# Two more groups of a down projection by seven block products, and the up projection's products grouped by length

## The chip, the cores and the metric

One core of a Trainium2 chip. The metric is the device time in microseconds (us) of one execution of the whole two-layer trunk; the median of several runs counts.

## What is computed

Each of two layers projects the normalised input into three attention branches (stick-breaking, forgetting, and a sparse one over selected keys), gates and mixes them, and adds them to the residual stream. The change touches only what follows in each layer, the feed-forward part, and one load at the very end:

```
h2 = _rmsnorm(x, g_mlp)
x = x + jnp.square(jax.nn.relu(h2 @ w_up)) @ w_down
...
return _rmsnorm(x, g_final)
```

There are 256 tokens, 1024 model columns and 4096 hidden columns, all float32.

## The kernel before, in words

**Products.** A float32 operand is split into a rounded part (hi) and its rest (lo). ScalarE writes hi (L92) and VectorE subtracts it (L93); both results go into rings of four buffers each, `whi` and `wlo`, of 128 x 1024. A full product is `mm3` (L120 to L122): hi by hi, hi by lo and lo by hi, three matmuls. Weights arrive in a ring of four `raw` tiles of 1 MB, loaded by SyncE's queue.

**Up projection** (`up_mm`, L708 and L709). The 4096 hidden columns are taken in 16 groups c of 256, each of two blocks of 128. A block gets its own PSUM bank. For each of eight slices k of the contraction, the weight's hi multiplies the input's hi and lo at once (512 columns, L708), and the weight's lo multiplies the input's hi (256 columns, L709), added into the second half of the bank. Then `up_part` adds the two halves (ScalarE copies one, VectorE adds the other, L681) and applies relu and square; the bank is free when VectorE's L681 is done. `up_done` splits the result. Banks of the name `mm` are a ring of three; the first two groups take three `mm` and one `av`. Their order on TensorE is written out by hand (`manual_schedule`); everything else is put in order by a scheduler when the program is built, and each engine then runs its own queue strictly in that order.

**Down projection.** A group c < `NS` is done by `down_seven`: its 256 tokens x 256 hidden x 1024 columns are a product of 2 x 2 block matrices, done as seven block products (`ORDER`) in place of eight. For that, VectorE forms four sums of the activations in `up_done` (L694 to L697) and splits a 128 x 896 tile (L702), and in `down_seven` forms four combinations of the weights in a tile `T` (L754 to L756), of which there is one buffer, and then splits seven half-rows of 512 columns where an ordinary group has four. The seven sums are gathered in banks p1 to p7 by all groups. The other groups are done by `down_half`, four slices of 128 and 512 output columns at a time: column half 0 goes into banks p4 and p2, half 1 into p8 and p3. I call a `down_seven` call a **seven** (21 matmuls of 512 columns) and a `down_half` call a **half** (24 of them).

```
items = sorted([((c + 0.5) / NS, down_seven, (c,)) for c in range(NS)] +
               [((q + 1) / (8 - NS // 2), down_half, (q, 0)) for q in range(8 - NS // 2)], key=lambda t: t[0])
```

This list is the first pass: with `NS = 6`, six sevens and the five halves of column half 0, interleaved by their fractions. Then `down_sum` combines p1 to p7 on ScalarE and VectorE while TensorE runs the halves of column half 1, and the last lines add to the residual, square it for the final norm, scale and store. `gfb`, the final gain, is loaded in the last layer just before the first pass.

Of the kernel before, what the change touches and what calls it, by code (L numbers as in the profile page):

```python
# [9 lines left out]
F32 = mybir.dt.float32  # L10
# [5 lines left out]
T, D, DEPTH, COLS, DFF = 256, 1024, 2, 7244, 4096  # L16
# [5 lines left out]
EPS = 1e-6  # L22
NEG = -1.0e38
GONE = -3.0e38
NS = 6
TWO_PI = 6.283185307179586


def AP(src, off, dims):
    return bass.AP(tensor=src.tensor, offset=src.offset + off, ap=[list(d) for d in dims])  # L30
# [3 lines left out]
def trunk_kernel(ctx: ExitStack, tc: tile.TileContext, x, positions, g_mix, w_in, b_forget, w_branch,  # L34
                 w_out, g_mlp, w_up, w_down, g_final, out):
    nc = tc.nc
    act, dve, pool, pe, dma = nc.scalar, nc.vector, nc.gpsimd, nc.tensor, nc.sync
# [3 lines left out]
    tp2 = ctx.enter_context(tc.tile_pool(name="t2", bufs=1))  # L41
# [6 lines left out]
    def at_tile(name="at"):  # L48
        return ps.tile([128, 512], F32, name=name, tag="at", bufs=2)
# [35 lines left out]
    def split(raw, k, n, steps=1):  # L85
        hi = wp.tile([128, 1024], F32R, name="whi", tag="whi", bufs=4)
        lo = wp.tile([128, 1024], F32R, name="wlo", tag="wlo", bufs=4)
        h3 = hi[:, :k * n].rearrange("p (k n) -> p k n", k=k)
        l3 = lo[:, :k * n].rearrange("p (k n) -> p k n", k=k)
        m = k // steps  # L90
        for i in range(0, k, m):
            act.activation(h3[:, i:i + m], raw[:, i:i + m], AF.Copy)  # L92
            dve.tensor_sub(l3[:, i:i + m], raw[:, i:i + m], h3[:, i:i + m].bitcast(F32))  # L93
        return h3, l3

    def raw_tile(k, n):
        raw = wp.tile([128, 2048], F32, name="raw", tag="raw", bufs=4)
        return raw[:, :k * n].rearrange("p (k n) -> p k n", k=k)

    def w_rows(src, off, rs, k0, n, loads=1):  # L100

        raw = raw_tile(4, n)
        m = 4 // loads
        for i in range(0, 4, m):
            dma.dma_start(raw[:, i:i + m, :], AP(src, off + (k0 + i) * 128 * rs, [[rs, 128], [128 * rs, m], [1, n]]))
        r = []
        for q in range(2):
            h, l = split(raw[:, 2 * q:2 * q + 2, :], 2, n, 2 if loads == 4 and q == 0 else 1)
            r += [(h[:, i, :], l[:, i, :]) for i in range(2)]
        return r  # L110
# [7 lines left out]
    def mm3(o, a, b, start, stop):  # L118
        (ah, al), (bh, bl) = a, b
        pe.matmul(o, ah, bh, start=start, stop=False)  # L120
        pe.matmul(o, ah, bl, start=False, stop=False)  # L121
        pe.matmul(o, al, bh, start=False, stop=stop)  # L122
# [9 lines left out]
    def blk(tiles, k, c0=0, c1=256, p0=0, p1=128):  # L132
        h, l = tiles[k // 2][:2]
        return h[p0:p1, k % 2, c0:c1], l[p0:p1, k % 2, c0:c1]
# [50 lines left out]
    def rstd_of(ss):  # L185
        n = ss.shape[1]
        ms = small.tile([128, 2], F32, name="ms")[:, :n]
        pool.tensor_add(ms, ss[:, :, 0], ss[:, :, 1])  # L188
        pool.tensor_scalar(ms, ms, 1.0 / D, EPS, op0=OP.mult, op1=OP.add)
        r = small.tile([128, 2], F32, name="rstd")[:, :n]  # L190
        pool.tensor_tensor(r, ms, mhalf[:, :n], op=OP.pow)
        return r
# [25 lines left out]
    for layer in range(DEPTH):  # L218
# [8 lines left out]
        with tc.tile_pool(name=f"att{layer}", bufs=1, reuse_waits="tile") as att:  # L227
# [110 lines left out]
            for n, c in enumerate((KI, KC, KC + 64)):  # L338
# [3 lines left out]
                p = at_tile("kT")  # L342
                for j in range(2):
                    pe.transpose(p[:, j * 128:j * 128 + 128], kdup[:, j, n, :], ident)
                hi, lo = kh[:, n, :], kl[:, n, :]
# [12 lines left out]
            for j, c, n in SEG:  # L358
                for h in range(4):
                    z = at_tile("zi")  # L360
                    i = h % 2
# [56 lines left out]
            p = at_tile("cum")  # L418
# [10 lines left out]
            p = at_tile("cumt")  # L429
# [238 lines left out]
        with tc.tile_pool(name=f"mlp{layer}", bufs=1, reuse_waits="tile") as mlp:  # L668
            sq, uT = {}, {}
# [15 lines left out]
            def up_done(c):  # L685

                u = sq[c]
                if c >= NS:
                    hi, lo = [mlp.tile([128, 2, 256], F32R, name=f"u{t}{c}") for t in "hl"]
# [14 lines left out]
            def up_mm(o, wb, ks):  # L704

                h, l = wb
                for k in ks:
                    pe.matmul(o, h[:, k, :], xt[k // 2][2][:, :, k % 2, :], start=k == 0, stop=False)  # L708
                    pe.matmul(o[:, 256:512], l[:, k, :], blk(xt, k)[0], start=False, stop=k == 7)  # L709

            first = []
# [2 lines left out]
            for ks in (range(4), range(4, 8)):  # L714
                for n, (o, w) in enumerate(first):
                    up_mm(o, w, ks)
                    if n == 0 and not ks[0]:
                        part(1)
                    if ks[0]:
                        up_part(n // 2, n % 2, [o])  # L720
                        if n % 2:
                            up_done(n // 2)
# [19 lines left out]
            def add(p, a, b, stop):  # L742
                if p not in prod:
                    prod[p] = BANK[p](f"p{p}")
                mm3(prod[p], a, b, p not in opened, stop)
                opened.add(p)

            def down_seven(c):

                raw = raw_tile(2, 1024)  # L750
                dma.dma_start(raw, AP(w_down, (layer * DFF + c * 256) * D, [[D, 128], [128 * D, 2], [1, D]]))
                r4 = raw.rearrange("p k (h n) -> p k h n", h=2)
                t = mlp.tile([128, 4, 512], F32, name="T", tag="T", bufs=1)
                dve.tensor_sub(t[:, 0:2], r4[:, :, 1, :], r4[:, 0])  # L754
                dve.tensor_sub(t[:, 2], r4[:, 1, 1, :], t[:, 0])
                dve.tensor_sub(t[:, 3], r4[:, 1, 0, :], t[:, 2])  # L756
                right = []
                for v in (r4[:, 0, 0:1, :], r4[:, 1], t[:, 0:2], t[:, 2:4]):
                    k = v.shape[1]
                    h, l = split(v, k, 512)  # L760
                    right += [(h[:, i], l[:, i]) for i in range(k)]
                hi, lo = uT[c]
                for p, f, w in ORDER:
                    add(p, (hi[:, f], lo[:, f]), right[w], c == NS - 1 and p in (1, 5, 6, 7))

            def down_half(q, cg):

                c = NS + 2 * q
                ws = w_rows(w_down, layer * DFF * D + cg * 512, D, 2 * c, 512)
                end = c == 14  # L770
                order = [(i, j) for i in range(4) for j in range(2)]
                if end and cg and layer == DEPTH - 1:
                    order = [(i, j) for j in range(2) for i in range(4)]
                for i, j in order:
                    add(((4, 2), (8, 3))[cg][j], blk(uT, 2 * c + i, j * 128, j * 128 + 128), ws[i], end and i == 3)

            def down_sum():

# [12 lines left out]

            last = layer == DEPTH - 1
            if last:
                gfb = mlp.tile([128, D], F32, name="gfb")
                dma.dma_start(gfb, AP(g_final, 0, [[0, 128], [1, D]]))
                ss = small.tile([128, 2, 2], F32, name="ss")
            else:
                xt, ss, part = norm_in(layer * 8 + 8, (at_tile, pt_tile))
            items = sorted([((c + 0.5) / NS, down_seven, (c,)) for c in range(NS)] +
                           [((q + 1) / (8 - NS // 2), down_half, (q, 0)) for q in range(8 - NS // 2)], key=lambda t: t[0])  # L800
            for _, f, args in items:
                f(*args)
            for cg in range(2):
                if cg == 0:
                    down_sum()
                else:
                    for q in range(8 - NS // 2):
                        down_half(q, 1)
                    o = prod[8], prod[3]
                for j in range(2):  # L810
                    if cg:
                        dve.scalar_tensor_tensor(xs[j][cg], o[j], r2[:, j:j + 1], xs[j][cg], op0=OP.mult, op1=OP.add)
                    if last:
                        junk = small.tile([128, 512], mybir.dt.bfloat16, name="junk", tag="junk", bufs=1)
                        act.activation(junk, xs[j][cg], AF.Square, accum_out=ss[:, j, cg:cg + 1])
                        dve.tensor_mul(xs[j][cg], xs[j][cg], gfb[:, cg * 512:cg * 512 + 512])
                if not last:
                    part(cg)
                for j in range(2):
                    if last and cg == 1:  # L820
                        rl = rstd_of(ss[:, j:j + 1, :])
                        act.activation(xs[j][1], xs[j][1], AF.Copy, scale=rl)
                        dma.dma_start(AP(out, j * 128 * D + 512, [[D, 128], [1, 512]]), xs[j][1])
                        dve.tensor_scalar(xs[j][0], xs[j][0], rl, None, op0=OP.mult)
                        dma.dma_start(AP(out, j * 128 * D, [[D, 128], [1, 512]]), xs[j][0])
# [23 lines left out]
```

## Time and profile before

| | us |
|---|---|
| median of 3 runs (lowest, highest) | 882.96 (881.09, 884.18) |
| the profiled execution | 881.56 |
| its span, first to last instruction | 879.7 |
| TensorE busy in it | 862.7 (98%) |
| VectorE busy | 695.4 (79%) |
| ScalarE busy | 591.1 (67%) |

The profile is of one execution. PE is TensorE's matmuls, PEld its weight loads, DVE VectorE, ACT ScalarE, POOL GpSimd, SP the load queue. In the timeline, the first number is the start of an instruction in us from the span's start and the second its duration; the brackets give the engine's idle time before it and who ended it. Matmuls overlap in their pipeline, so the distance between two starts, not a duration, says what one costs.

### The profile page before, as it was taken

The numbers are of one execution on the slowest core, as the hardware profiler recorded it, in microseconds if no ns is written. First come the engines' busy times: TensorE is split into PE (matmuls) and PEld (weight loads), VectorE is DVE, ScalarE is ACT, GpSimd is POOL, SyncE is SP. The second block draws the span as 40 slices with busy tenths as digits, with TensorE's granted clock in tenths as the row PEclk, the third lists the DMA queues.
The fourth block names the chain that finished last, engine by engine and source line by source line (L and its number), as shares of the span: only waits on it lengthen the run. The fifth ranks groups of instructions, "written<-read, shape, count | busy, mean of one in ns | idle before, by whom it ended". The sixth has DMA issues, their size and how long they took to land.

```text
span 879.7 us, 13066 instructions
## 1 busy us (share of the span) xinstructions
PE 862.7 (98%) x4794; PEld 753.7 (86%) x4794; DVE 695.4 (79%) x1156; ACT 591.1 (67%) x996; POOL 114.0 (13%) x216
## 2 busy tenths in 40 slices
PE   7999999999999999999999999999999999999996
PEld 7998998888888888878899989988888888888784
DVE  5899787988667977888668987789777598778892
ACT  6766886777557877755466758677755588775552
POOL 2300331334001000000011014032510100000001
PEclk9999999999999999999999999999999999999998
DMA  8744544354555665456466363454256555545531
GB/s 295 247 145 144 192 144 144 101 187 144 171 181 176 192 191 192 154 188 233 148 203 201 133 200 137 144 180 133 95 167 212 195 192 189 180 159 191 191 144 49
DMA packets 99408, 150.92 MB, mean 172 GB/s; under 512 B 2928, under 2 KB 58256, under 8 KB 99344
## 3 DMA queue, kind: packets, MB, share of 16 engines
q1 hardware_dynamic: 99344, 150.08, 52.1%
q8 instruction: 38, 0.62, 0.3%
q14 instruction: 26, 0.21, 0.1%
HBM read 149.02 MB, written 1.05 MB: 171 GB/s over the span
## 4 chain that ended last, share of the span: by engine, by line
PE 92%; DVE 4%; ACT 1%; issue 1%; DMA 1%; SPq 0%; POOL 0%; POOLq 0%; ACTq 0%
PE mm L121 13%; PE mm L120 13%; PE mm L122 13%; PE mm L708 13%; PE mm L709 7%; PE p L121 6%; PE p L122 6%; PE p L120 6%; PE av L457 2%; PE pT L441 2%; PE at L121 1%; PE at L122 1%; PE at L120 1%; DVE wlo L93 1%; DVE qs L148 1%; PE xtp L171 1%
## 5 line engine op out<-in xcount | busy, mean ns | idle before, releaser
L93 DVE TENSOR_TENSOR wlo<-raw,whi 128x1024 fp32r<-128x1024 f32 (+4 forms) x289 | 339.8, 1183 | 95.6 <-ACT whi L92 94.1
L92 ACT ACTIVATE whi<-raw 128x1024 fp32r<-128x1024 f32 (+4 forms) x289 | 291.7, 1016 | 146.6 <-PE mm L122 48.7
L708 PE MATMUL mm<-xT,whi 128*128 128x512 f32 x496 | 174.7, 396 | 0.3 <-DVE sq L681 0.3
L709 PE MATMUL mm<-xT,wlo 128*128 128x256 f32 x496 | 139.1, 280 | 0.0
L121 PE MATMUL mm<-wlo,xT 128*128 128x512 f32 (+2 forms) x320 | 122.6, 384 | 0.5 <-DVE wlo L93 0.5
L122 PE MATMUL mm<-whi,xT 128*128 128x512 f32 (+2 forms) x320 | 121.4, 382 | 0.0
L120 PE MATMUL mm<-whi,xT 128*128 128x512 f32 (+2 forms) x320 | 119.1, 383 | 0.5 <-ACT xT L176 0.5
L708 PEld LDWEIGHTS mm<-xT,whi 128*128 128x128 f32 x496 | 93.0, 188 | 22.8 <-PE mm L709 0.9
L709 PEld LDWEIGHTS mm<-xT,wlo 128*128 128x128 f32 x496 | 93.7, 189 | 0.1
L122 PE MATMUL mm<-xT,wlo 128*128 128x256 f32 x256 | 73.6, 287 | 0.0
L120 PE MATMUL mm<-xT,whi 128*128 128x256 f32 x256 | 73.2, 286 | 0.0
L121 PE MATMUL mm<-xT,whi 128*128 128x256 f32 x256 | 73.2, 286 | 0.0
L120 PEld LDWEIGHTS mm<-whi,xT 128*128 128x128 f32 x320 | 60.8, 190 | 10.4 <-ACT xT L176 0.9
L121 PEld LDWEIGHTS mm<-wlo,xT 128*128 128x128 f32 x320 | 60.9, 190 | 10.3 <-DVE wlo L93 1.4
L122 PEld LDWEIGHTS mm<-whi,xT 128*128 128x128 f32 x320 | 60.7, 190 | 9.1
L188 POOL TENSOR_TENSOR ms<-ss 128x2 f32<-128x2 f32 (+1 forms) x6 | 4.3, 718 | 466.2 <-ACT junk L181 292.8
L122 PE MATMUL p<-whi,ul 128*128 128x512 f32 x160 | 62.4, 390 | 0.0
L121 PE MATMUL p<-wlo,uh 128*128 128x512 f32 x160 | 62.3, 389 | 0.0
L120 PE MATMUL p<-whi,uh 128*128 128x512 f32 x160 | 60.1, 391 | 0.4 <-ACT whi L92 0.4
L92 ACT ACTIVATE whi<-T 128x1024 fp32r<-128x1024 f32 x24 | 25.4, 1060 | 38.7 <-PE p L122 16.1
L120 PEld LDWEIGHTS mm<-xT,whi 128*128 128x128 f32 x256 | 49.0, 191 | 0.1
L121 PEld LDWEIGHTS mm<-xT,whi 128*128 128x128 f32 x256 | 49.0, 191 | 0.1
(245 smaller groups left out, 1734.5 us busy)
## 6 DMA issues: line engine op xcount, KB each, us to landing
raw<-in_w_in_dram SPq DMA_DIRECT2D x48, 1024.0 KB, 5.0
raw<-in_w_up_dram SPq DMA_DIRECT2D x32, 1024.0 KB, 5.1
raw<-in_w_down_dram SPq DMA_DIRECT2D x32, 1024.0 KB, 5.0
raw<-in_w_branch_dram SPq DMA_DIRECT2D x12, 1024.0 KB, 5.0
raw<-in_w_out_dram SPq DMA_DIRECT2D x8, 1024.0 KB, 5.0
raw<-in_w_in_dram SPq DMA_DIRECT2D x8, 736.0 KB, 5.0
raw<-in_w_in_dram SPq DMA_DIRECT2D x3, 728.0 KB, 4.3
out_dram<-x SPq DMA_DIRECT2D x4, 256.0 KB, 2.2
```

What stands on the lines that cost most here:

```text
L92: act.activation(h3[:, i:i + m], raw[:, i:i + m], AF.Copy)
L93: dve.tensor_sub(l3[:, i:i + m], raw[:, i:i + m], h3[:, i:i + m].bitcast(F32))
L120: pe.matmul(o, ah, bh, start=start, stop=False)
L121: pe.matmul(o, ah, bl, start=False, stop=False)
L122: pe.matmul(o, al, bh, start=False, stop=stop)
L148: dve.scalar_tensor_tensor(dst[half(1 - i), :, i, :], src[half(i)], scale, dst[half(i), :, i, :].bitcast(F32), op0=OP.mult, op1=OP.subtract)
L171: pe.transpose(p[:, i * 256 + j * 128:i * 256 + j * 128 + 128], xs[j][h][:, c:c + 128], ident)
L188: pool.tensor_add(ms, ss[:, :, 0], ss[:, :, 1])
L441: pe.transpose(p[:, q * 128:q * 128 + 128], e[:, i, q * 128:q * 128 + 128], ident)
L457: pe.matmul(o[:, c + c0:c + 256], v, p[:, a:b], start=s == 0 and n == 0, stop=s == 1 and n == 1)
L708: pe.matmul(o, h[:, k, :], xt[k // 2][2][:, :, k % 2, :], start=k == 0, stop=False)
L709: pe.matmul(o[:, 256:512], l[:, k, :], blk(xt, k)[0], start=False, stop=k == 7)
```

## The change

`NS` goes from 6 to 8: groups 6 and 7 become sevens, and a half less is left in each column half (four and four in place of five and five). The divisor of the halves' fractions goes from `8 - NS // 2` to `9 - NS // 2`, so the first pass ends with a seven, and the flags that close the sums move accordingly. In `up_mm`, the eight 512-column products of a bank come first and then the eight of 256 columns (for the first two groups, whose contraction is done in two parts, four and four). `gfb` moves out of the feed-forward pool into a buffer of the input tiles' ring, behind the up projection's last use of it.

```diff
-NS = 6
+NS = 8
...
                 h, l = wb
                 for k in ks:
                     pe.matmul(o, h[:, k, :], xt[k // 2][2][:, :, k % 2, :], start=k == 0, stop=False)
+                for k in ks:
                     pe.matmul(o[:, 256:512], l[:, k, :], blk(xt, k)[0], start=False, stop=k == 7)
...
                 for p, f, w in ORDER:
-                    add(p, (hi[:, f], lo[:, f]), right[w], c == NS - 1 and p in (1, 5, 6, 7))
+                    add(p, (hi[:, f], lo[:, f]), right[w], c == NS - 1 and p != 3)
...
-                    add(((4, 2), (8, 3))[cg][j], blk(uT, 2 * c + i, j * 128, j * 128 + 128), ws[i], end and i == 3)
+                    add(((4, 2), (8, 3))[cg][j], blk(uT, 2 * c + i, j * 128, j * 128 + 128), ws[i], cg == 1 and end and i == 3)
...
             if last:
-                gfb = mlp.tile([128, D], F32, name="gfb")
-                dma.dma_start(gfb, AP(g_final, 0, [[0, 128], [1, D]]))
                 ss = small.tile([128, 2, 2], F32, name="ss")
...
             items = sorted([((c + 0.5) / NS, down_seven, (c,)) for c in range(NS)] +
-                           [((q + 1) / (8 - NS // 2), down_half, (q, 0)) for q in range(8 - NS // 2)], key=lambda t: t[0])
+                           [((q + 1) / (9 - NS // 2), down_half, (q, 0)) for q in range(8 - NS // 2)], key=lambda t: t[0])
             for _, f, args in items:
                 f(*args)
+            if last:
+                gfb = tp2.tile([128, D], F32, name="gfb", tag="xT", bufs=4)
+                dma.dma_start(gfb, AP(g_final, 0, [[0, 128], [1, D]]))
```

The built programs show where instructions stand. First place: SyncE's queue in the first layer's first pass, which gives the order of the groups. L751 (L752 in the changed kernel) is the load of a seven, 128x2x1024; L105 is that of a half. Before:

```order
L751 DMA raw_3942<-in_w_down_dram 128x2x1024
L105 DMA raw_3992<-in_w_down_dram 128x4x512
L751 DMA raw_4026<-in_w_down_dram 128x2x1024
L105 DMA raw_4069<-in_w_down_dram 128x4x512
L751 DMA raw_4103<-in_w_down_dram 128x2x1024
L751 DMA raw_4146<-in_w_down_dram 128x2x1024
L105 DMA raw_4189<-in_w_down_dram 128x4x512
L751 DMA raw_4223<-in_w_down_dram 128x2x1024
L105 DMA raw_4266<-in_w_down_dram 128x4x512
L751 DMA raw_4300<-in_w_down_dram 128x2x1024
L105 DMA raw_4343<-in_w_down_dram 128x4x512
```

The same queue in the changed program:

```order
L752 DMA raw_3950<-in_w_down_dram 128x2x1024
L752 DMA raw_4000<-in_w_down_dram 128x2x1024
L105 DMA raw_4043<-in_w_down_dram 128x4x512
L752 DMA raw_4077<-in_w_down_dram 128x2x1024
L105 DMA raw_4120<-in_w_down_dram 128x4x512
L752 DMA raw_4154<-in_w_down_dram 128x2x1024
L752 DMA raw_4197<-in_w_down_dram 128x2x1024
L105 DMA raw_4240<-in_w_down_dram 128x4x512
L752 DMA raw_4274<-in_w_down_dram 128x2x1024
L105 DMA raw_4317<-in_w_down_dram 128x4x512
L752 DMA raw_4351<-in_w_down_dram 128x2x1024
L752 DMA raw_4394<-in_w_down_dram 128x2x1024
```

Before, two sevens follow each other once in the pass; in the changed program three times, at its start, in the middle and at its end.

Second place: VectorE's queue early in the first layer's up projection. `mm_3154` and `mm_3171` are the banks of group 2 and `mm_3213` that of the first block of group 3; the second block of group 3 takes the ring's bank of `mm_3154` again. `wlo_3324` belongs to group 5's weights and takes the ring's buffer of `wlo_3206`, which the product in `mm_3213` reads. Before:

```order
L93 TENSOR_TENSOR wlo_3269<-raw_3262,whi_3268 128x1024
L697 TENSOR_TENSOR sq_3118<-sq_3118 128x128
L681 TENSOR_TENSOR sq_3188<-mm_3154,sq_3188 128x256
L681 TENSOR_TENSOR sq_3188<-mm_3171,sq_3188 128x256
L93 TENSOR_TENSOR wlo_3324<-raw_3321,whi_3323 128x1024
L702 TENSOR_TENSOR fl1_3140<-sq_3118,fh1_3139 128x896
```

The same stretch in the changed program:

```order
L93 TENSOR_TENSOR wlo_3269<-raw_3262,whi_3268 128x1024
L697 TENSOR_TENSOR sq_3118<-sq_3118 128x128
L702 TENSOR_TENSOR fl0_3107<-sq_3085,fh0_3106 128x896
L93 TENSOR_TENSOR wlo_3324<-raw_3321,whi_3323 128x1024
L702 TENSOR_TENSOR fl1_3140<-sq_3118,fh1_3139 128x896
L681 TENSOR_TENSOR sq_3188<-mm_3154,sq_3188 128x256
L681 TENSOR_TENSOR sq_3188<-mm_3171,sq_3188 128x256
L681 TENSOR_TENSOR sq_3247<-mm_3213,sq_3247 128x256
```

The additions that free the banks (L681) stood ahead of the split of `wlo_3324` and now stand behind it and behind the split of `fl1_3140`. The second layer's queue has the same order.

## Rows read from the trace of the kernel before

**Rows 1.** The page: the chain that ended last, share of the span by engine.

```profile
PE 92%; DVE 4%; ACT 1%; issue 1%; DMA 1%; SPq 0%; POOL 0%; POOLq 0%; ACTq 0%
```

**Rows 2.** Timeline of PE (start, us, engine, line, operation), second layer's last halves.

```profile
858.23 0.39 PE L120 MATMUL p<-whi,uh 128*128 128x512 f32 x1
...
860.95 0.39 PE L122 MATMUL p<-whi,ul 128*128 128x512 f32 x1
```

**Rows 3.** Timeline of PE, up projection, 512 and 256 columns alternating.

```profile
319.62 0.39 PE L708 MATMUL mm<-xT,whi 128*128 128x512 f32 x1
...
323.08 0.39 PE L708 MATMUL mm<-xT,whi 128*128 128x512 f32 x1
```

**Rows 4.** Timeline of PE, a run of 256-column matmuls alone.

```profile
61.26 0.28 PE L120 MATMUL mm<-xT,whi 128*128 128x256 f32 x1
...
62.93 0.28 PE L122 MATMUL mm<-xT,wlo 128*128 128x256 f32 x1
```

**Rows 5.** Timeline of PE, the second of two adjacent sevens.

```profile
382.44 0.39 PE L121 MATMUL p<-wlo,fh 128*128 128x512 f32 x1
...
384.88 0.73 PE L120 MATMUL p<-whi,fh 128*128 128x512 f32 x2 [0.56 <-ACT whi L92]
...
386.47 0.40 PE L122 MATMUL p<-whi,fl 128*128 128x512 f32 x1
```

**Rows 6.** Timeline of DVE, one seven and one half.

```profile
386.00 1.22 DVE L93 TENSOR_TENSOR wlo<-raw,whi 128x1024 fp32r<-128x1024 f32 x1
...
394.78 1.22 DVE L93 TENSOR_TENSOR wlo<-T,whi 128x1024 fp32r<-128x1024 f32 x1 [1.21 <-ACT whi L92]
395.92 1.22 DVE L93 TENSOR_TENSOR wlo<-raw,whi 128x1024 fp32r<-128x1024 f32 x1
```

**Rows 7.** Timeline of PE, up projection, from group 3's first block to its second.

```profile
282.41 0.40 PE L708 MATMUL mm<-xT,whi 128*128 128x512 f32 x1
...
285.12 0.28 PE L709 MATMUL mm<-xT,wlo 128*128 128x256 f32 x1
285.56 0.47 PE L708 MATMUL mm<-xT,whi 128*128 128x512 f32 x1 [0.16 <-DVE sq L681]
```

**Rows 8.** Timeline of DVE, the same place.

```profile
285.00 0.74 DVE L681 TENSOR_TENSOR sq<-mm,sq 128x256 f32<-128x256 f32 x2
286.42 1.23 DVE L93 TENSOR_TENSOR wlo<-raw,whi 128x1024 fp32r<-128x1024 f32 x1 [0.67 <-ACT whi L92]
287.56 1.09 DVE L702 TENSOR_TENSOR fl<-sq,fh 128x896 fp32r<-128x896 f32 x1
288.56 0.29 DVE L694 TENSOR_TENSOR sq<-sq 128x128 f32<-128x128 f32 x1
289.16 0.42 DVE L681 TENSOR_TENSOR sq<-mm,sq 128x256 f32<-128x256 f32 x1
```

**Rows 9.** Timeline of ACT, the same place.

```profile
285.32 1.06 ACT L92 ACTIVATE whi<-raw 128x1024 fp32r<-128x1024 f32 x1 [1.09 <-PE mm L708]
```

**Rows 10.** Busy time by stretch (us; PE, PEld, DVE, ACT, POOL; PEclk, DMA, GB/s), the end.

```profile
871.40:874.00 2.60, 0.00 (x0) 0.00 (x0) 1.22 (x3) 1.45 (x3) 0.53 (x2) 1.00 0.27 102
874.00:877.00 3.00, 0.00 (x0) 0.00 (x0) 1.10 (x2) 0.72 (x1) 1.41 (x3) 0.52 0.25 94
```

**Rows 11.** Timeline of PE, the program's start: 364-column matmuls.

```profile
12.46 0.51 PE L121 MATMUL mm<-wlo,xT 128*128 128x364 f32 x1
...
13.96 0.34 PE L122 MATMUL mm<-whi,xT 128*128 128x364 f32 x1
14.14 0.33 PE L120 MATMUL mm<-whi,xT 128*128 128x364 f32 x1
```

**Rows 12.** Timeline of DVE and PE, the end of the program.

```profile
870.92 0.39 PE L122 MATMUL p<-whi,ul 128*128 128x512 f32 x1
871.93 0.49 DVE L824 TENSOR_SCALAR x<-x,rstd 128x512 f32<-128x512 f32 x1 [1.00 <-POOL rstd L191]
872.33 0.74 DVE L812 SCALAR_TENSOR_TENSOR x<-p,r,x 128x512 f32<-128x512 f32 x1
```

## The prediction

> **What bounds the kernel now.** I read the chain of work that ended last first: 92% of it is TensorE [rows 1]. So a change is worth what it does to the stream of matmuls: how many there are, how far apart they start, and where the stream stops. The timeline of TensorE gives the spacing. In the last halves twelve steps take from 858.23 to 860.95, so a 512-column matmul costs 0.227 us [rows 2]. A seven is then 21 x 0.227 = 4.77 us of TensorE, a half 24 x 0.227 = 5.45. In the up projection ten pairs of 512 and 256 columns take from 319.62 to 323.08, 0.346 a pair [rows 3].
>
> The stream stops in two places that the change touches. In the first pass of the down projection, at the second of two adjacent sevens, ten steps take from 382.44 to 386.47, which is 4.03 instead of 2.27: 1.76 us are lost, and the bracket names ScalarE's copy `whi` [rows 5]. Why there? VectorE needs 386.00 to 395.92 for one half and one seven [rows 6]. The half's part is two splits of 1.14 each (394.78 to 395.92), so the seven takes VectorE 9.92 - 2.28 = 7.64 us, of which 1.21 is a wait for ScalarE's copy of `T`, which exists once. A seven thus takes VectorE 7.64 and TensorE 4.77; a half takes VectorE 2.28 and TensorE 5.45. Alternating, TensorE is just the slower (10.22 against 9.92). Two sevens in a row let it run into VectorE. The other place is group 3 of the up projection: the second block's first matmul starts at 285.56, where 285.24 was possible (285.12 plus the 0.12 of a 256-column step), and it waited for L681 to free its bank [rows 4, 7].
>
> **The change, part by part.**
>
> *Fewer products.* Two groups in each layer go from 24 to 21 matmuls: six fewer in each layer, 6 x 0.227 = 1.36 us. All of them stood on TensorE's path. The Trainium skill (TensorE: Matmul & The Clock Gate, section Back-to-back issue gap) gives about 131 ns for a 512-column matmul in a sustained stream with weight loads; by that estimate the saving would be 0.79 in each layer and the forecast 1.1 us longer. The trace has 227, and the measurement decides.
>
> *Grouping by length.* Fourteen 256-column matmuls alone take from 61.26 to 62.93, 0.119 each [rows 4]. A pair taken apart is 0.227 + 0.119 = 0.346, exactly the 0.346 of the alternating pair. I cost the grouping at zero. Bounds: the steps vary by 2 or 3 ns, and over 256 pairs in each layer that is 0.7 either way.
>
> *The first pass.* The load queue shows the order. Where sevens were adjacent once, they now are three times. The pair in the middle and the pair at the end have the neighbours of today's (half, seven, seven, half), so each should cost the 1.76 of [rows 5]; the first follows the up projection, whose end prepares the first seven as it does now, and I take 1.76 for it too. That is 5.3 in place of 1.76: 3.5 more, less the 1.36 saved, **+2.2 in each layer**. The bound below is VectorE's own need: seven sevens (the first is prepared in the up projection, before and after) and four halves are 7 x 7.64 + 4 x 2.28 = 62.6, against TensorE's 8 x 4.77 + 4 x 5.45 = 60.0, so at least 2.6 are lost, +(2.6 - 1.76 - 1.36) = -0.5. The bound above is the whole surplus at each pair, 3 x (7.64 - 4.77) = 8.6, +5.5. I take the pairs because a like pair stands in the trace. Before, the same count gives 5 x 7.64 + 5 x 2.28 = 49.6 for VectorE against 55.9, so there it had slack; now it has none.
>
> *The up projection.* This is not in the diff, but in VectorE's queue. L681 for `mm_3154`, which frees the bank that group 3's second block needs, now stands behind the split `wlo_3324` and the split `fl1`. `wlo_3324` cannot begin before the buffer of `wlo_3206` is free, and that one is read to the end of the very product before the waiting one. So: that product's last matmul starts at 285.12 and takes 0.28, ending at 285.40 as now. ScalarE's copy, which now begins at 285.32, when the product's last 512-column matmul is done [rows 9], can begin about 0.9 earlier, since in the grouped order eight 256-column matmuls follow that one; it ends at about 285.5. VectorE then does the split, 1.14 (286.42 to 287.56), `fl1`, 1.00 (287.56 to 288.56), and L681, 0.42 [rows 8]: 285.55 + 2.56 = 288.1, and TensorE starts at about 288.2 instead of 285.24. That is 3.0 lost where 0.3 is lost today: **+2.7 in each layer**. Bounds: if VectorE starts at 285.40, +2.4; if ScalarE's copy keeps its time and the split stays at 286.42, the end is 288.98, +3.5. Nothing gives it back, since TensorE remains the slower engine in the rest of the up projection and behind it.
>
> *What costs nothing.* Groups 6 and 7 need four sums and a longer split on VectorE and ScalarE in the up projection, as groups 0 to 5 do now; TensorE covers them there with 16 x 0.346 = 5.5 us in each group. If that cover were gone, the longer split would cost at most its own 1.00 [rows 8] a group. `down_sum` keeps four halves (21.8 us) behind it in place of five. The load of `gfb` moves down the load queue, where its own wait, the end of the up projection, is past before the load behind it is due. At the end, the eviction of p3 (L812) today starts at 872.33 behind a scaling that waited 1.00 for POOL; it now stands ahead of that scaling, but ScalarE's squares still stand behind the same wait. I take zero, with 1.0 either way [rows 12].
>
> **The sum.** 2 x (2.2 + 2.7) = 9.8 us longer. The profiled execution took 881.56, so it would become 891.4; it stands 1.4 below the median of 882.96, and against the median the forecast is **892.8 us**.
>
> **The rivals.**
>
> *The clock falls in the new gap.* Today's last matmul starts at 870.92 and is done at 871.31; the granted clock is 1.00 in the stretch to 874.00 and 0.52 in the next 3.00, so it fell to its lower level, 1.2 GHz, at about 874.1, after 2.8 us without matmuls [rows 10, 12]. The gap of 3.0 in each up projection is as long. The stop in [rows 5], 0.56 idle in one piece, left it at its upper level (0.227 steps go on behind it). At the start, the 364-column matmuls from 12.46 to 13.96 are 0.30 apart at the lower level, and 0.18 after the rise [rows 11], so time at that level loses some 40%. How long it would stay there no row shows: at least the 1.5 us of those rows, at most the 14 us to the rise, so 0.6 to 5.6 a gap. Near the lower end, 2 a gap, this gives 892.8 + 4 = 896.8. The Trainium skill (the same page, Part 1) calls the throttled state the default, released by activity; by that rule this rival would happen, but no run here shows a gap between matmuls that long.
>
> *Faster.* The pairs cost nothing, because VectorE enters the pass with a lead. The place is the second seven of each pair, the price 1.76; it decides if VectorE is ahead by more than 7.64 - 4.77 = 2.9 us when a pair begins. If the bank were also freed in time in the up projection, 2 x (1.36 + 1.76) = 6.2 would be gained: 876.7. For it: VectorE waits in this pass, so it has room. Against it: those waits are for ScalarE's copy of the one `T` [rows 6], the ring of four holds one seven, and the queue order in the up projection does not depend on the lead.
>
> *Little is lost in the first pass.* Only the lower bound holds there: 2 x (2.7 - 0.5) = 4.4, 887.4. For it: one slow pair may leave VectorE no further behind at the next. Against it: today's pair loses 1.76 although VectorE has slack over the pass.
>
> *The whole surplus at each pair:* 2 x (2.7 + 5.5) = 16.4, 899.4. Against it: in today's pair 1.1 of the 2.9 is absorbed.
>
> *The products are not fewer.* The built program excludes it; the count is 12 down.
>
> **How the numbers follow.** The forecast has 0.60, the clock 0.20, little lost 0.08, the whole surplus 0.05, faster 0.04; 0.03 is left for a mixture that ends within 0.3% of the median, which is about what a measurement of this kernel can tell from no change (880.3 to 885.6). The range of 888 to 899 leaves out the two cases below, the one near no change, and the longest; it takes in the bounds of the up projection and most of those of the pass and of the clock. Faster 0.04, same 0.03, slower 0.93.
>
> **What would show it.** In the profile after: twelve fewer matmuls in all; in each up projection one gap before a first L708 of about 3 us, ended by L681 on VectorE, with `wlo` and `fl` on VectorE just before; in each first pass three places of about 1.8 us lost, ended by ScalarE's `whi`; pair and 512 spacing as now. A granted clock of 0.5 behind the gap shows the rival. The forecast is wrong if L681 ends within a microsecond of the product ahead, or if the first pass is no longer than 60 us.

## The result, and the profile after

The changed kernel took **893.26 us** (median of 4 runs, 891.21 to 893.47) against 882.06 for the kernel before in the same comparison: a ratio of 1.0123, 95% interval 1.0107 to 1.0139. It is 11.2 us slower. The forecast was 892.8, that is 9.8 us more than the 882.96 known then.

In the profiled executions the span went from 879.72 to 891.64. The table gives, for the profiled execution of every run of this study, the distance in us from the first to the last start of the up projection's matmuls, and of the matmuls into p1 to p8 (first pass and the rest of the down projection), each by layer. The runs e1 to e7 are described below.

| kernel | up, layer 1 | up, layer 2 | down, layer 1 | down, layer 2 |
|---|---|---|---|---|
| before | 90.27 | 91.59 | 85.71 | 84.84 |
| after | 93.27 | 94.83 | 88.26 | 87.38 |
| e1, grouping only | 93.27 | 93.27 | 85.67 | 84.80 |
| e2, eight sevens only | 91.60 | 91.58 | 89.44 | 88.54 |
| e3, group 2 ungrouped | 90.48 | 90.48 | 88.27 | 87.37 |
| e4, no combinations | 94.80 | 94.83 | 82.29 | 81.40 |
| e5, six alternating | 91.59 | 91.58 | 83.69 | 82.80 |
| e6, the same, grouped | 90.51 | 90.50 | 83.65 | 82.76 |
| e7, eight spread out | 90.51 | 90.50 | 82.77 | 82.75 |

From before to after: up +3.00 and +3.24, down +2.55 and +2.54, together 11.3 of the 11.9 us by which the span grew; the rest is some 0.3 each at the program's start and end.

The chain that ended last, where TensorE had 92% [rows 1], now runs through VectorE:

```profile
PE 78%; DVE 14%; ACT 3%; issue 2%; DMA 1%; SPq 0%; POOL 0%; POOLq 0%; ACTq 0%; DVEq 0%
```

**The gap in the up projection.** The timeline of TensorE, where [rows 7] had 285.56:

```profile
282.50 2.00 PE L708 MATMUL mm<-xT,whi 128*128 128x512 f32 x8
284.35 1.11 PE L710 MATMUL mm<-xT,wlo 128*128 128x256 f32 x8
288.35 0.93 PE L708 MATMUL mm<-xT,whi 128*128 128x512 f32 x3 [2.89 <-DVE sq L681]
```

ScalarE's queue, where [rows 9] had the copy `whi` at 285.32:

```profile
284.55 1.06 ACT L92 ACTIVATE whi<-raw 128x1024 fp32r<-128x1024 f32 x1 [0.89 <-PE mm L708]
285.51 0.93 ACT L701 ACTIVATE fh<-sq 128x896 fp32r<-128x896 f32 x1
286.35 0.64 ACT L680 ACTIVATE sq<-mm 128x256 f32<-128x256 f32 x2
```

And VectorE, where [rows 8] had L681 first:

```profile
284.19 1.08 DVE L702 TENSOR_TENSOR fl<-sq,fh 128x896 fp32r<-128x896 f32 x1
285.64 1.23 DVE L93 TENSOR_TENSOR wlo<-raw,whi 128x1024 fp32r<-128x1024 f32 x1 [0.36 <-ACT whi L92]
286.78 1.08 DVE L702 TENSOR_TENSOR fl<-sq,fh 128x896 fp32r<-128x896 f32 x1
287.78 1.08 DVE L681 TENSOR_TENSOR sq<-mm,sq 128x256 f32<-128x256 f32 x3
```

The eight short matmuls run from 284.35 and end at 285.46, and ScalarE's copy ends at 285.61. The split `wlo` needs both and starts at 285.64. `fl` and the three L681 follow, and TensorE starts at 288.35, after 2.89 us idle. The step over the gap is 3.17 (from a start at 285.18) where a short matmul costs 0.12: 3.05 lost, against 0.32 before.

ScalarE's queue has changed with VectorE's. L681 adds what ScalarE has copied in L680. Before, the two L680 stood ahead of the copy `whi`:

```profile
283.58 0.66 ACT L680 ACTIVATE sq<-mm 128x256 f32<-128x256 f32 x2
```

Now they stand behind `whi` and `fh` and are done only at 286.99. VectorE's own queue holds L681 longer, to 287.78, so it sets the gap; but with VectorE's order alone put back, L681 would still have waited for these copies.

**The adjacent sevens.** What TensorE waited for, in us, times and longest, before:

```profile
PE p L120 <- ACT whi L92: 1.6, 4, 0.6
...
PE mm L708 <- DVE sq L681: 0.3, 2, 0.2
```

and after:

```profile
PE mm L708 <- DVE sq L681: 5.8, 2, 2.9
PE p L120 <- ACT whi L92: 5.3, 16, 0.6
```

Four idle stretches for ScalarE's copy, two in each layer, have become sixteen, eight in each layer. The first pair of the first layer has two of them:

```profile
367.07 0.74 PE L120 MATMUL p<-whi,fh 128*128 128x512 f32 x2 [0.47 <-ACT whi L92]
368.02 0.50 PE L120 MATMUL p<-whi,uh 128*128 128x512 f32 x1 [0.21 <-ACT whi L92]
```

The middle pair and the last have three each. In the middle pair, the first stretch has no like in [rows 5] and the other two have:

```profile
391.08 0.74 PE L120 MATMUL p<-whi,fh 128*128 128x512 f32 x2 [0.23 <-ACT whi L92]
...
394.56 0.73 PE L120 MATMUL p<-whi,fh 128*128 128x512 f32 x2 [0.58 <-ACT whi L92]
395.50 0.50 PE L120 MATMUL p<-whi,uh 128*128 128x512 f32 x1 [0.22 <-ACT whi L92]
```

VectorE has the same period for a half and a seven, 395.68 to 405.60, 9.92 us, as in [rows 6]:

```profile
395.68 1.22 DVE L93 TENSOR_TENSOR wlo<-raw,whi 128x1024 fp32r<-128x1024 f32 x1
...
404.45 1.22 DVE L93 TENSOR_TENSOR wlo<-T,whi 128x1024 fp32r<-128x1024 f32 x1 [1.21 <-ACT whi L92]
405.60 1.22 DVE L93 TENSOR_TENSOR wlo<-raw,whi 128x1024 fp32r<-128x1024 f32 x1
```

**The clock.** Busy time by stretch (us; PE, PEld, DVE, ACT, POOL; granted clock, DMA share, GB/s), around the second layer's gap:

```profile
720.80:723.70 2.90, 0.02 (x1) 0.03 (x1) 2.70 (x4) 1.93 (x5) 0.00 (x0) 1.00 1.01 306
723.70:724.10 0.40, 0.39 (x2) 0.36 (x3) 0.40 (x2) 0.18 (x1) 0.00 (x0) 1.00 0.76 264
724.10:727.50 3.40, 3.40 (x11) 2.72 (x10) 1.26 (x6) 2.22 (x4) 0.00 (x0) 0.50 0.03 6
```

Granted clock 0.50 is the lower of TensorE's two levels, 1.2 GHz. The clock fell 0.4 us after the matmuls had begun again at 723.71. In the first layer's gap, as long, it did not:

```profile
285.40:288.30 2.90, 0.06 (x1) 0.00 (x0) 2.66 (x4) 1.93 (x5) 0.00 (x0) 1.00 1.00 316
288.30:292.00 3.70, 3.65 (x20) 3.21 (x21) 1.56 (x7) 2.30 (x5) 0.00 (x0) 1.00 0.07 24
```

The two up projections have the same gap (3.17 us from start to start) and are 93.27 and 94.83 long; the fall cost 1.56.

### The profile page after: what moved, and what is told of

It reads as the page before. It is cut to its first block, busy times and chain, and to the rows that moved or that the text cites. A ratio compares the mean times of both kernels' runs of the same rounds, so it can differ in the third digit from the quotient of the medians.

```text
span 891.6 us, 13108 instructions
## 1 busy us (share of the span) xinstructions
PE 864.7 (97%) x4782; PEld 751.9 (84%) x4782; DVE 716.9 (80%) x1192; ACT 597.4 (67%) x1004; POOL 114.0 (13%) x216
## 3 DMA queue, kind: packets, MB, share of 16 engines
HBM read 149.02 MB, written 1.05 MB: 168 GB/s over the span
## 4 chain that ended last, share of the span: by engine, by line
PE 78%; DVE 14%; ACT 3%; issue 2%; DMA 1%; SPq 0%; POOL 0%; POOLq 0%; ACTq 0%; DVEq 0%
PE mm L121 13%; PE mm L120 13%; PE mm L122 13%; PE mm L708 13%; DVE wlo L93 8%; PE mm L710 6%; PE av L457 2%; ACT whi L92 2%; PE p L121 2%; PE p L122 2%; PE p L120 2%; PE pT L441 2%; DVE T L755 2%; PE at L121 1%; PE at L122 1%
## 5 line engine op out<-in xcount | busy, mean ns | idle before, releaser
L708 PE MATMUL mm<-xT,whi 128*128 128x512 f32 x496 | 126.9, 396 | 5.8 <-DVE sq L681 5.8
L708 PEld LDWEIGHTS mm<-xT,whi 128*128 128x128 f32 x496 | 89.6, 190 | 22.0 <-issue 6.1
L122 PE MATMUL mm<-xT,wlo 128*128 128x256 f32 x256 | 73.6, 287 | 0.0
L710 PEld LDWEIGHTS mm<-xT,wlo 128*128 128x128 f32 x496 | 68.9, 191 | 5.5
L710 PE MATMUL mm<-xT,wlo 128*128 128x256 f32 x496 | 70.3, 283 | 0.0
L92 ACT ACTIVATE whi<-T 128x1024 fp32r<-128x1024 f32 x32 | 33.9, 1059 | 53.5 <-DVE T L757 31.4
L93 DVE TENSOR_TENSOR wlo<-T,whi 128x1024 fp32r<-128x1024 f32 x32 | 39.1, 1222 | 18.6 <-ACT whi L92 18.6
L121 PE MATMUL p<-wlo,uh 128*128 128x512 f32 x128 | 50.0, 390 | 0.0
L122 PE MATMUL p<-whi,ul 128*128 128x512 f32 x128 | 49.9, 390 | 0.0
L120 PEld LDWEIGHTS mm<-xT,whi 128*128 128x128 f32 x256 | 49.0, 191 | 0.1
L121 PEld LDWEIGHTS mm<-xT,whi 128*128 128x128 f32 x256 | 49.0, 191 | 0.1
```

## The experiments

**e1: the grouping alone.** The kernel before, with only this edit:

```diff
                     pe.matmul(o, h[:, k, :], xt[k // 2][2][:, :, k % 2, :], start=k == 0, stop=False)
+                for k in ks:
                     pe.matmul(o[:, 256:512], l[:, k, :], blk(xt, k)[0], start=False, stop=k == 7)
```

> Six sevens as before, only the up projection's products grouped by length. Theory (the wait is made by the grouping: with it the scheduler puts L681 behind the split of wlo and the split of fl on VectorE): each up projection has the gap of about 3.0 us at group 3's second block, the first passes keep one slow pair, so +2.7 to +3.2 a layer, 887.5 to 888.5 us. Rival (the wait comes from groups 6 and 7, whose activations give VectorE more to do): no gap above 0.5 us, 882 us. Rival (grouped matmuls themselves are dearer): no gap, but a pair of 512 and 256 columns above 0.346 us, some 883 to 886.

Measured: 887.32 us, before 881.21; ratio 1.0070 (1.0047 to 1.0094). The waits of TensorE:

```profile
PE mm L708 <- DVE sq L681: 5.8, 2, 2.9
...
PE p L120 <- ACT whi L92: 1.6, 4, 0.6
```

This is 0.2 below the range I gave. Both gaps of 2.9 are there, with six sevens: the grouping makes them, and the activations of groups 6 and 7 have no part in it. The down projection is as before (85.67, 84.80). The clock held in both layers of the profiled execution, and both up projections are 93.27 long. That execution took 885.68 us at a mean granted clock of 0.998; the other three took 887.13 to 888.90 at 0.992 to 0.995. So the clock may have fallen in their gaps, but no trace of them was kept.

**e2: the eight sevens alone.** The changed kernel with the alternating order of products put back (the edit of e1 reversed).

> Eight sevens as in the changed kernel, the up projection's products alternating as before. Theory (the down projection's part is the adjacent sevens, VectorE 7.64 us against TensorE 4.77): three slow pairs in each first pass, no gap of 3 us in the up projection; +2.2 to +2.6 a layer, 886.5 to 887.5 us, and more if the first pair is not prepared as well as in the changed kernel, up to 890. Rival (both parts hang together, the wait in the up projection is made by the longer splits): the gap is there too, 892 to 893. Rival (twelve matmuls fewer is all that counts): 879.3.

Measured: 888.80 us, before 881.21; ratio 1.0090 (1.0056 to 1.0123). The waits:

```profile
PE p L120 <- ACT whi L92: 6.7, 16, 1.2
...
PE mm L708 <- DVE sq L681: 0.3, 2, 0.2
```

No gap in the up projection, three slow pairs in each pass. The down projection is 3.7 longer than before in each layer, 1.2 more than in the changed kernel: the first pair is dearer here, as the timeline of TensorE shows (1.15 idle, where the changed kernel has 0.47 at the same matmul).

```profile
362.24 0.40 PE L122 MATMUL p<-whi,fl 128*128 128x512 f32 x1
363.79 0.73 PE L120 MATMUL p<-whi,fh 128*128 128x512 f32 x2 [1.15 <-ACT whi L92]
```

So each of the two parts slows the kernel down by itself: 1.0070 and 1.0090, where both together give 1.0123.

**e3: group 2 ungrouped.** The changed kernel; `up_mm` gets a flag that makes it alternate, and it is set for one group of the main loop:

```diff
-                    up_mm(os[-1], w, range(8))
+                    up_mm(os[-1], w, range(8), c < 3)
```

> The changed kernel, but the products of group 2 alone (two of 32 blocks of each up projection) alternate again. Theory (queue order): L681 stands ahead of the split again, the gap of 3.0 us goes in both layers, and the granted clock stays at its upper level through the second up projection; 893.3 - 2 x 3.0 - about 1 = 886.3 to 887.5 us. Rival (grouping is dear in itself, or the gap is set by something else than the queue): a sixteenth of it undone, 892.5 to 893.3, the gap stays.

Measured: 885.71 us, before 881.21; ratio 1.0050 (1.0030 to 1.0069). VectorE and then TensorE at the place of the gap:

```profile
283.39 0.75 DVE L681 TENSOR_TENSOR sq<-mm,sq 128x256 f32<-128x256 f32 x2
284.06 1.22 DVE L93 TENSOR_TENSOR wlo<-raw,whi 128x1024 fp32r<-128x1024 f32 x1
```

```profile
282.93 0.87 PE L712 MATMUL mm<-xT,wlo 128*128 128x256 f32 x6
283.96 0.70 PE L708 MATMUL mm<-xT,whi 128*128 128x512 f32 x2 [0.15 <-DVE sq L681]
```

L681 is ahead of the split again and the idle time is 0.15 in place of 2.89. Two of 32 blocks put back in their old order bring the first up projection from 93.27 to 90.48; the down projection keeps its loss. So the order of the queues makes the gap, and grouped products by themselves do not. VectorE's queue and ScalarE's are not told apart here: the two L680 are ahead of the copy `whi` again as well.

```profile
281.97 0.66 ACT L680 ACTIVATE sq<-mm 128x256 f32<-128x256 f32 x2
282.90 1.06 ACT L92 ACTIVATE whi<-raw 128x1024 fp32r<-128x1024 f32 x1 [0.27 <-PE mm L708]
```

The time is 0.6 below the range I gave. That range started from 893.3, of a comparison in which the kernel before took 882.06; it took 881.21 in this one.

**e4: no combinations.** The changed kernel without L755 to L757; it leaves out the combinations of the weights, and its output is another one:

```diff
-                t = mlp.tile([128, 4, 512], F32, name="T", tag="T", bufs=1)
-                dve.tensor_sub(t[:, 0:2], r4[:, :, 1, :], r4[:, :, 0])
-                dve.tensor_sub(t[:, 2], r4[:, 1, 1, :], t[:, 0])
-                dve.tensor_sub(t[:, 3], r4[:, 1, 0, :], t[:, 2])
...
-                for v in (r4[:, 0, 0:1, :], r4[:, 1], t[:, 0:2], t[:, 2:4]):
+                for v in (r4[:, 0, 0:1, :], r4[:, 1], r4[:, :, 1, :], r4[:, :, 0, :]):
```

> The changed kernel without the four combinations of the weights in down_seven (L755 to L757): the seven splits are made from the raw weights, so 2.34 us of VectorE and the one buffer T go from each seven; what is left out is part of the seven products' right sides. Theory (VectorE's 7.64 us and its wait for the copy of T make the slow pairs): the pairs go, no wait above 0.5 us in the first pass, about 5.5 us less in each layer, 881.5 to 883.5. Rival (the ring of four buffers holds just one seven, so adjacent sevens wait whatever VectorE does): the pairs keep 1 us or more each, 887 to 892.

Measured: 880.24 us, before 881.21; ratio 0.9990 (0.9975 to 1.0006), 1.3 below the range I gave. The list of TensorE's waits has no entry for ScalarE's copy any more; its longest is the gap, which this kernel keeps:

```profile
PE mm L708 <- DVE sq L681: 5.8, 2, 2.9
```

The down projection is 82.29 and 81.40, 5.97 and 5.98 less than after, with the same 360 matmuls and the same ring of four. The rival with the ring falls: what makes an adjacent pair slow is VectorE's work on the combinations and the wait around `T`. (This run takes away the work and the buffer together; which of the two counts for more was not tried.) Counted matmul by matmul against this kernel, the changed one falls behind by 1.35 us at the first pair of the first layer, 2.34 at the middle one and 2.28 at the last, and elsewhere by no more than 0.1.

The clock fell in both gaps of this run, and both up projections are 94.8 long; the first layer's stretch:

```profile
288.10:291.40 3.30, 3.30 (x13) 2.95 (x12) 1.86 (x5) 2.15 (x4) 0.00 (x0) 0.50 0.00 0
```

**e5: six sevens that alternate.** The changed kernel with `NS = 6` and the alternating order of products; the new divisor stays, so against the kernel before the order of groups differs by this:

```diff
-                           [((q + 1) / (8 - NS // 2), down_half, (q, 0)) for q in range(8 - NS // 2)], key=lambda t: t[0])
+                           [((q + 1) / (9 - NS // 2), down_half, (q, 0)) for q in range(8 - NS // 2)], key=lambda t: t[0])
```

> Six sevens again and the up projection's products alternating as before, but the changed kernel's other parts kept: the divisor 9 - NS // 2, the closing flags and the place of gfb. With six sevens and five halves the new divisor lets them alternate without a break, so no two sevens are adjacent. Theory (each adjacent pair of sevens costs 1.8 us, and seven and half in turn cost nothing): no slow pair, first pass and halves of column half 1 together 1.8 us shorter in each layer than before, 877.5 to 878.5 us where before has 881 to 882. Rival (VectorE's total in the pass is what counts, not who stands beside whom): six sevens are the same total, so 881 to 882.

Measured: 877.54 us, before 881.41; ratio 0.9957 (0.9942 to 0.9971). The only wait between the first up projection matmul and the last down projection one in a layer is the old small one:

```profile
PE mm L708 <- DVE sq L681: 0.3, 2, 0.2
```

The same six sevens, the same five halves, in another order: the down projection is 2.02 and 2.04 shorter than before. So what stands beside a seven decides, and not VectorE's total.

**e6: the same, grouped except group 2.** Shown against the changed kernel; `up_mm` has the flag of e3:

```diff
-NS = 8
+NS = 6
...
-                    up_mm(os[-1], w, range(8))
+                    up_mm(os[-1], w, range(8), c < 3)
```

> As the run with six alternating sevens, and the up projection's products grouped by length except for group 2. Theory (the grouping is neutral once the queue order of L681 is repaired): equal to the ungrouped one within 1 us, 877.5 to 878.5; if grouping holds the pair at 0.3495 us where the alternating order takes 0.3465 in some up projections and 0.3535 in others, it lies between -1 and +0.8 us a layer of it. Rival (grouping costs TensorE something of its own): over 880.

Measured: **875.62 us**, before 881.41; ratio 0.9935 (0.9919 to 0.9950), the lowest median of this study. Against e5 it is 1.9 us less, and the up projections are 1.08 less each: 90.51 and 90.50 against 91.59 and 91.58. That is more than the 1 us a layer of my second case; the first one, equal times, did not come true. The timeline of e5 has four alternating pairs from 319.79 to 321.21, 0.355 each:

```profile
319.79 0.40 PE L708 MATMUL mm<-xT,whi 128*128 128x512 f32 x1
...
321.21 0.40 PE L708 MATMUL mm<-xT,whi 128*128 128x512 f32 x1
```

and that of e6 eight grouped ones from 320.01 to 322.80, 0.349 each:

```profile
320.01 2.00 PE L708 MATMUL mm<-xT,whi 128*128 128x512 f32 x8
321.85 1.11 PE L712 MATMUL mm<-xT,wlo 128*128 128x256 f32 x8
322.80 2.00 PE L708 MATMUL mm<-xT,whi 128*128 128x512 f32 x8
```

The two times' intervals overlap at the edge; it is the profiles that separate the two orders.

**e7: eight sevens, spread out.** As e3, with the first pass written out: seven, seven, half, seven, half, seven, half, seven, half, seven, half, seven, half, seven, the last two of the halves being of column half 1:

```diff
-            items = sorted([((c + 0.5) / NS, down_seven, (c,)) for c in range(NS)] +
-                           [((q + 1) / (9 - NS // 2), down_half, (q, 0)) for q in range(8 - NS // 2)], key=lambda t: t[0])
-            for _, f, args in items:
+            items = [(down_seven, (0,)), (down_seven, (1,)), (down_half, (0, 0)), (down_seven, (2,)), (down_half, (1, 0)), (down_seven, (3,)), (down_half, (2, 0)), (down_seven, (4,)), (down_half, (3, 0)), (down_seven, (5,)), (down_half, (0, 1)), (down_seven, (6,)), (down_half, (1, 1)), (down_seven, (7,))]
+            for f, args in items:
...
-                    for q in range(8 - NS // 2):
+                    for q in range(2, 8 - NS // 2):
```

> Eight sevens, group 2 of the up projection alternating and the others grouped, and two of the four halves of column half 1 brought forward into the first pass, so that only the first two sevens are adjacent. Theory (pairs cost, not the number of sevens): one slow pair of about 1.2 us in each layer, first pass and rest 2 to 3 us shorter in each layer than before; of that some is given back at the end of each layer, where only two halves are left to cover down_sum: 878.5 to 880 us. Rival (eight sevens are more than VectorE can feed in any order): the waits of about 5.5 us in each layer come back at other places, 885 to 887.

Measured: 877.39 us, before 881.41; ratio 0.9951 (0.9936 to 0.9966), 1.1 below the range I gave. Eight sevens can be fed but for the first pair. That pair is in the waits, with a new one behind `down_sum`:

```profile
PE p L120 <- ACT whi L92: 1.3, 4, 0.4
...
PE xtp L171 <- DVE x L815: 0.5, 1, 0.5
```

The down projection is 82.77 in the first layer, 0.9 below that of e6; but from its last matmul to the next up projection's first there are 256.04 us (438.73 to 694.77) against 253.74 in e6 (437.18 to 690.92), 2.3 more. Of these, 0.9 have only moved: the eight transposes for the next layer that e6 runs among its halves stand behind them in e7. First e6, then e7:

```profile
423.60 1.04 PE L171 MATMUL xtp<-ident,x 128*128 128x128 f32 x8
```

```profile
438.96 1.04 PE L171 MATMUL xtp<-ident,x 128*128 128x128 f32 x8
```

The other 1.4 are lost, with two halves to cover `down_sum` instead of five: VectorE is still at it, to 439.60, when the last half's last matmul starts at 438.73.

```profile
438.86 0.74 DVE L793 SCALAR_TENSOR_TENSOR x<-T,r,x 128x512 f32<-128x512 f32 x1
```

TensorE's two waits right behind, 0.40 for ScalarE's L176 and 0.49 for VectorE's L815, are 0.9 of the 1.4. In the second layer, which has no such transposes, both down projections are alike (82.75 and 82.76): what the fewer products save, the first pair takes. So eight sevens did not come out ahead of six here.

## Why the prediction was right, and where its sizes were off

*The gap in the up projection: right.* Forecast 3.0 lost for 0.3, +2.7 a layer; measured 3.05 for 0.32, +2.73. It was read from the queue order and four durations, and putting the order back removed it (e3). I followed VectorE's queue alone. ScalarE's had moved too, which did not change the sum, since it was done first (286.99 against 287.78).

*Fewer products: right.* Forecast 1.36 a layer; e4 and e5 have no waits in the down projection, and differ by 83.69 - 82.29 = 1.40.

*The adjacent sevens: right in kind, undersized.* I took 1.76 for each pair. Before against e5, one pair costs 85.71 - 83.69 = 2.02, so the stretch that I read in [rows 5] left out 0.26. After against e4, three cost 5.97, but they are not alike: 1.35, 2.34 and 2.28. I had too much for the first and too little for the other two, and the errors partly cancel, which is luck. The step "3.5 more, less the 1.36 saved" gave +2.2, and 2.55 was measured: 0.35 a layer too little. The bound below, VectorE's own need, was not it. The first pair is not the same in every program either: it loses 1.2 more in e2, where only the order of the up projection's products differs; the cause of that was not followed further.

*The grouping: not zero.* "Exactly the 0.346 of the alternating pair" held for the stretch that I read, in before's first up projection, which is 90.27 long. Its second is 91.59, and so are those of e2 and e5; grouped ones are 90.5 without a gap. Grouping is worth about 1.1 us in five of the six alternating up projections and costs 0.2 in the sixth, and the bound of 0.7 either way was too narrow. In the changed kernel the gap hides it: the second up projection would otherwise have grown by 2.73 + 1.56, and grew by 3.24.

*The clock: a rival that came true in part.* It fell in one of the two gaps, at 1.56, within the 0.6 to 5.6 that I gave and near the 2 I used. The Trainium skill (TensorE: Matmul & The Clock Gate, Part 1) has the throttled state as the default that activity releases. The traces agree in part: the clock fell behind three of the six such gaps and held behind the other three. That it is at its lower level at the start I read from spacings alone (0.30 and 0.18, [rows 11]).

*The end, at zero with 1.0 either way:* 0.3 longer.

So the sum of 9.8 holds 2 x 2.7 that was right, 2 x 0.35 too little for the pairs, and three terms at zero that measured -0.8 (grouping: +0.27 in the first layer, -1.05 in the second), +1.56 (clock) and +0.6 (start and end). Together that is the 11.9 of the profiled executions. The forecast of 892.8 lies within 0.5 of the 893.26 measured, and part of this is luck: grouping and clock offset each other in part, and the kernel before came out at 882.06 in the comparison, 0.9 below the median that I started from.

## What to carry to other kernels

Saving matmuls paid here only where the engine that prepares their operands kept up group by group, not in the sum: put the groups that it is slow at beside those that it is fast at, and count its time for each kind of group. An edit that only reorders one engine's work can move the queues of others; read where the instruction that frees a bank now stands, and what those ahead of it wait for, on every engine that it needs. Try the parts of such a change alone: here each of them was slower by itself. The grouping became a gain once group 2 kept its old order (e6 against e5). The two further sevens lost most of their cost once they were spread out, but brought no gain over six (e7 against e6).

## What was not expected of the hardware

Matmuls of 512 and 256 columns in turn have two spacings, even in one up projection. In before's first, seven pairs from 282.41 [rows 7] to the next row take 0.354 us each; behind the short stop at 285.56 they take 0.3465, to its end [rows 3].

```profile
284.89 0.40 PE L708 MATMUL mm<-xT,whi 128*128 128x512 f32 x1
```

The other five up projections that alternate throughout have the same stop and stay near 0.353 behind it; the alternating group 2 of e3, e6 and e7 has 0.347. Grouped pairs took 0.349 to 0.351 wherever the clock held. What picks one of the two was not found.

The granted clock fell behind three of the six gaps of 2.9 us in the profiled executions (one of two in after, none in e1, both in e4), though each gap stands between the same instructions and TensorE was busy up to it. Each fall made the up projection about 1.5 us longer (94.8 against 93.27).
